# A three-layer transformer block whose instruction order is sorted with another machine model

## The chip, the cores and the metric

The kernel runs on one core of a Trainium2 chip. The metric is the time of one execution on the device, in microseconds (us). A core has five engines that work side by side, each with a queue of its own that it serves in order: PE (matrix products, fed by the weight loads PEld), DVE (elementwise work and reductions), ACT (functions of one operand, copies), POOL (here a few powers and fills) and SP, which issues almost all transfers from the main memory. The engines wait for each other by semaphores.

## The reference

The input is 256 tokens of width 1024. Three layers follow one another, each a mixer and a feed-forward network, all in fp32.

```python
def reference(x, c, ...):
    x = first_block(x, c, w_ada, ...)   # 1 layer
    return second_block(x, p_2, ...)    # 2 layers

# first_block
mod = silu(c) @ w_ada + b_ada                    # 6 x 1024 modulation values
mix = token_mixer(x * (1 + sc1) + sh1)           # top-64 indexer attention (8 heads) + gated convolution
x = layer_norm(ALPHA * x + g1 * mix)
ff = (silu(h @ w_gate) * (h @ w_up)) @ w_down    # h = x * (1 + sc2) + sh2, hidden width 2816
x = layer_norm(ALPHA * x + g2 * ff)

# second_block, layers i = 0 (gla_mixer) and i = 1 (diff_attn_mixer)
h = h + mixer_i(rms_norm(h))
h = h + swiglu_2(rms_norm(h))
h = h + sigmoid(rms_norm(h) @ ple_w_gate[i]) * (p[i] @ ple_w_proj[i])
```

The first mixer scores all keys for each query, keeps 64 of them and attends to these. The second is a gated linear attention in four heads with a forward and a backward direction. The third is an attention whose heads are differences of two softmaxes.

## The kernel before

The tokens stand in two tiles of 128 rows. Every large product streams its weight matrix once from the main memory in pieces of 256 to 512 KB. `stage` (L127 to L131) transfers a piece into one of 11 buffers `st` through SP's queue (L130). `gran` (L141 to L154) splits it into a high part `wh` (rounded copy on ACT, L150) and a low part `wl` (difference on DVE, L151); the pool `wp` has five buffers of each. The activations are split and transposed in the same way (class `XT`, `xh` and `xl`). `mm3` (L157 to L162) then makes three products for each pair of blocks: high by high (L159), high by low (L160), low by high (L162), accumulated in a bank of the result memory, of which the pool `psp` has four with the tag mm and four with the tag acc. Small transposes go through PE as well (L124).

The program runs through these stages: the modulation and the first projections (`block1`, `piece`, `both_cols`), the top-k selection in eight rounds of maxima on DVE with convolution products set between the rounds, the first attention (`attn_p`, `attn_t`, `attn_o`), the output product and the layer norm, then `ffn` (gate and up, then down, in 11 chunks of 256 columns), `gla`, `tail_layer` with a second `ffn`, `diff`, and `tail_layer` with a third `ffn`. In `diff`, `heads` (L1202 and following) makes for each pair of heads the scores (L1208), their row maximum (L1211), the scaled negative of it (L1214), the exponentials (L1217) and the difference of the two softmaxes (L1224); the source sets these calls by hand between the parts of the projections. `diff_consts` (L1075 and following), called in the second `ffn`, loads the four vectors `lv` and makes the factor `nlam` of them (L1082 to L1088).

The order of the instructions is not the order of the source. `tile.TileContext` records the instructions and sorts them when it is left: it plays the program through on a model of the machine, and whenever the model can take an instruction for an engine, it gets, of those whose inputs are done and for whose output a buffer is free, the one that stands first in the source (one block of `block1` has a higher priority). So the model decides which instruction passes which, and which buffer a tile gets. On the chip each engine then serves its queue in the order that came out, and waits where an input is not there yet. The default model is the one of the library's functional simulator.

## Time and profile before

| | us |
|---|---|
| median of 3 runs | 1054.07 (1052.72 to 1056.53) |
| profiled execution | 1055.7 |
| its span, from the first instruction to the last | 1053.9 |
| PE busy | 1015.8 (96%) |
| PEld busy | 811.2 (77%) |
| DVE busy | 636.7 (60%) |
| ACT busy | 554.8 (53%) |
| POOL busy | 49.5 (5%) |

Matmuls overlap in the records: in the third feed-forward network 840 of them, most recorded with some 390 ns each, fill 184 us. A busy PE is therefore not PE at its fastest, and a PE that is idle in the records has lost time in any case. The granted clock tells at which of its two levels PE ran. DMA share is the mean busy share of the 16 transfer engines.

### The profile page before, as it was taken

The page shows a single profiled execution, that of the slowest core. Times are in us where ns is not written, and L with a number is a line of the kernel's source. Part 1 is how long each engine was busy: PE and PEld are TensorE (multiplying, and loading weights), DVE is VectorE, ACT ScalarE, POOL GpSimd, SP SyncE. Part 2 cuts the span into 40 slices and gives each one's busy share as a digit, 9 for nine tenths or more (in the row PEclk, how much of TensorE's full clock was granted, in tenths as well). Part 3 has the DMA queues.
Part 4 walks back from the last instruction along what each step waited for, and adds up shares of the span by engine and source line. Part 5 has one row for each costly group of instructions (what it writes and reads, how often), then busy time and mean ns, then how long its engine had stood idle before and what let it go on. Part 6 is the DMA issues. An engine that isn't in the chain of part 4 may idle for free.

```text
span 1053.9 us, 13554 instructions
## 1 busy us (share of the span) xinstructions
PE 1015.8 (96%) x4883; PEld 811.2 (77%) x4883; DVE 636.7 (60%) x1043; ACT 554.8 (53%) x895; POOL 49.5 (5%) x43
## 2 busy tenths in 40 slices
PE   6889999999999999998999999999998999999998
PEld 3666675888888778886888888888676788888886
DVE  2378468654556476556555556578786665555654
ACT  2355446544445477464544446566857554444643
POOL 0000100000000000000000000004040100000000
PEclk9999999999999999999999999999999999999999
DMA  9957587966657255254665667445443466666601
GB/s 292 395 202 264 219 306 226 293 195 183 195 182 225 60 183 180 80 166 144 205 190 184 186 195 262 143 134 169 129 126 104 127 204 192 183 191 186 240 0 40
DMA packets 131783, 194.48 MB, mean 185 GB/s; under 512 B 10578, under 2 KB 93662, under 8 KB 131716
## 3 DMA queue, kind: packets, MB, share of 16 engines
q1 hardware_dynamic: 130936, 193.21, 57.4%
q10 hardware_dynamic: 780, 0.40, 0.2%
q8 instruction: 38, 0.62, 0.2%
q14 instruction: 29, 0.24, 0.1%
HBM read 192.53 MB, written 1.05 MB: 184 GB/s over the span
## 4 chain that ended last, share of the span: by engine, by line
PE 82%; DVE 7%; ACT 4%; DMA 3%; issue 2%; POOL 1%; SPq 0%; ACTq 0%; DVEq 0%; POOLq 0%
PE mmb L162 17%; PE mmb L159 17%; PE mmb L160 17%; PE acb L162 7%; PE acb L159 7%; PE acb L160 7%; DVE wl L151 2%; PE mmb L124 2%; PE acb L124 1%; POOL rs L276 1%; PE acb L337 1%; ACT wh L150 1%; DMA st<-in_w_ada_dram 1%; ACT e L1217 1%; PE mmb L337 1%
## 5 line engine op out<-in xcount | busy, mean ns | idle before, releaser
L151 DVE TENSOR_TENSOR wl<-st,wh 128x1024 fp32r<-128x1024 f32 (+4 forms) x292 | 350.9, 1206 | 233.2 <-ACT wh L150 232.4
L150 ACT CAST wh<-st 128x1024 fp32r<-128x1024 f32 (+4 forms) x292 | 300.7, 1037 | 281.9 <-PE mmb L162 141.8
L159 PE MATMUL mmb<-wh,xh 128*128 128x512 f32 (+4 forms) x888 | 352.7, 399 | 6.8 <-ACT xh L390 4.5
L160 PE MATMUL mmb<-wl,xh 128*128 128x512 f32 (+4 forms) x888 | 347.1, 392 | 2.8 <-DVE wl L151 2.8
L162 PE MATMUL mmb<-wh,xl 128*128 128x512 f32 (+4 forms) x888 | 342.3, 391 | 1.5 <-DVE xl L184 0.6
L159 PEld LDWEIGHTS mmb<-wh,xh 128*128 128x128 f32 x888 | 169.2, 191 | 44.4 <-ACT xh L390 6.3
L162 PEld LDWEIGHTS mmb<-wh,xl 128*128 128x128 f32 x888 | 169.4, 191 | 39.5 <-DVE xl L191 3.1
L160 PEld LDWEIGHTS mmb<-wl,xh 128*128 128x128 f32 x888 | 169.5, 191 | 34.6 <-DVE wl L151 3.3
L159 PE MATMUL acb<-wh,hh 128*128 128x512 f32 x216 | 84.0, 389 | 0.0
L160 PE MATMUL acb<-wl,hh 128*128 128x512 f32 x216 | 84.0, 389 | 0.0
L162 PE MATMUL acb<-wh,hl 128*128 128x512 f32 x216 | 66.6, 389 | 0.0
L159 PEld LDWEIGHTS acb<-wh,hh 128*128 128x128 f32 x216 | 40.6, 188 | 8.4
L162 PEld LDWEIGHTS acb<-wh,hl 128*128 128x128 f32 x216 | 40.5, 188 | 8.4
L160 PEld LDWEIGHTS acb<-wl,hh 128*128 128x128 f32 x216 | 40.5, 188 | 8.4
L878 POOL TENSOR_TENSOR rsx<-rsx,mhalf 128x1 f32<-128x1 f32 x12 | 10.8, 899 | 467.2 <-DVE rsx L877 467.2
L824 ACT ACTIVATE sg<-mmb,rsx 128x256 f32<-128x256 f32 x44 | 20.7, 474 | 22.2 <-PE mmb L162 20.4
L276 POOL TENSOR_TENSOR rs<-rs,mhalf 128x8 f32<-128x8 f32 (+1 forms) x14 | 20.0, 1434 | 240.7 <-DVE rs L275 240.7
L151 DVE TENSOR_TENSOR wxl<-st,wxh 128x1024 fp32r<-128x1024 f32 x22 | 26.7, 1219 | 3.0 <-ACT wxh L150 3.0
L825 DVE SCALAR_TENSOR_TENSOR sg<-mmb,rsx,sg 128x256 f32<-128x256 f32 x44 | 20.8, 480 | 11.1 <-ACT sg L824 11.1
L150 ACT CAST wxh<-st 128x1024 fp32r<-128x1024 f32 x22 | 22.7, 1051 | 5.0 <-PE acb L162 3.0
L874 ACT ACTIVATE junk<-x 128x1024 f32<-128x1024 f32 x10 | 10.6, 1059 | 25.3 <-DVE x L867 23.8
L831 DVE TENSOR_TENSOR hl<-mmb,hh 128x512 fp32r<-128x512 f32 x33 | 22.6, 684 | 1.8 <-ACT hh L830 1.8
(311 smaller groups left out, 1065.7 us busy)
## 6 DMA issues: line engine op xcount, KB each, us to landing
st<-in_ffn_w_in_dram SPq DMA_DIRECT2D x176, 256.0 KB, 3.4
st<-in_ffn_w_out_dram SPq DMA_DIRECT2D x44, 512.0 KB, 4.0
st<-in_w_ada_dram SPq DMA_DIRECT2D x32, 512.0 KB, 5.2
st<-in_diff_w_in_dram SPq DMA_DIRECT2D x24, 512.0 KB, 4.0
st<-in_w_gate_dram SPq DMA_DIRECT2D x44, 256.0 KB, 4.6
st<-in_w_up_dram SPq DMA_DIRECT2D x44, 256.0 KB, 3.1
st<-in_w_down_dram SPq DMA_DIRECT2D x22, 512.0 KB, 3.8
st<-in_w_ada_dram SPq DMA_DIRECT2D x32, 256.0 KB, 5.3
```

Of the source, the lines that this page charges most:

```text
L124: T.transpose(o, i, ident)
L150: A.copy(h[:, :n], src)
L151: V.tensor_sub(l[:, :n], src, h[:, :n].bitcast(F32))
L159: T.matmul(p_, xh, wh, start=start, stop=False)
L160: T.matmul(p_, xh, wl, start=False, stop=False)
L162: T.matmul(p_, xl, wh, start=False, stop=stop)
L276: G.tensor_tensor(r[:, :n], r[:, :n], mhalf[:, :n], op=OP.pow)
L337: T.matmul(bk[32 * j:32 * j + 32, :n], cB[:, kb, :], sts[kb // k][:, kb % k * n:kb % k * n + n], start=kb < 4, stop=kb >= 4)
L824: A.activation(sg, ps[t][:, 0:256], AF.Silu, scale=rs[t])
L825: V.scalar_tensor_tensor(sg, ps[t][:, 256:512], rs[t], sg, op0=OP.mult, op1=OP.mult)
L831: V.tensor_sub(hl, tv, hh.bitcast(F32))
L878: G.tensor_tensor(r, r, mhalf[:, 0:1], op=OP.pow)
```

## The change

The context is opened with a switch that sets the model on which the scheduler plays the program: the library's simulation in time (TimelineSim), which prices instructions, queues and transfers with another set of laws than the default. Nothing else differs: the same instructions, the same transfers, the same pools and priorities.

```diff
@@ -1344,7 +1344,7 @@
         aps[n] = nc.dram_tensor(f"in_{n}_dram", a.shape, mybir.dt.from_np(a.dtype), kind="ExternalInput").ap()
     o = nc.dram_tensor("out_0_dram", (1, S, D), F32, kind="ExternalOutput").ap()
-    with tile.TileContext(nc) as tc:
+    with tile.TileContext(nc, schedule_with_timeline_sim=True) as tc:
         body(tc, aps, o)
     r = _run(nc, [arrays], core_ids=[0])
```

## Rows read from the trace of the kernel before

**Rows 1.** The page: span, and each engine's busy us, share and instructions.
```profile
span 1053.9 us, 13554 instructions
PE 1015.8 (96%) x4883; PEld 811.2 (77%) x4883; DVE 636.7 (60%) x1043; ACT 554.8 (53%) x895; POOL 49.5 (5%) x43
```

**Rows 2.** Busy us (and instructions) by stage: start:end, length, engines, clock, DMA.
```profile
0.00:26.00 26.00, 16.91 (x94) 9.64 (x94) 5.86 (x17) 6.67 (x11) 1.68 (x7) 1.00 0.92 291
26.00:184.00 158.00, 145.97 (x799) 103.09 (x799) 104.05 (x254) 79.09 (x156) 9.02 (x6) 0.97 0.77 269
184.00:342.00 158.00, 158.00 (x716) 130.51 (x715) 89.11 (x94) 77.01 (x94) 0.00 (x0) 1.00 0.68 213
342.00:500.00 158.00, 152.90 (x755) 125.70 (x754) 99.90 (x193) 93.68 (x156) 7.45 (x10) 0.98 0.44 137
500.00:685.00 185.00, 185.00 (x843) 152.45 (x843) 105.47 (x117) 92.46 (x118) 1.93 (x2) 1.00 0.63 194
685.00:843.00 158.00, 150.98 (x751) 120.50 (x751) 116.37 (x229) 106.17 (x231) 27.43 (x16) 0.99 0.43 132
843.00:1027.00 184.00, 184.00 (x840) 151.74 (x839) 103.24 (x113) 89.88 (x111) 0.54 (x1) 1.00 0.55 171
1027.00:1054.00 27.00, 22.04 (x97) 17.58 (x95) 12.72 (x30) 9.85 (x23) 1.46 (x1) 0.98 0.11 39
```

**Rows 3.** The same view of three stretches with the lower granted clock.
```profile
46.00:49.40 3.40, 3.40 (x11) 2.82 (x10) 2.02 (x4) 2.35 (x3) 0.00 (x0) 0.50 1.06 409
...
482.90:486.30 3.40, 3.40 (x10) 2.64 (x9) 0.34 (x1) 0.00 (x0) 0.00 (x0) 0.50 0.85 280
797.00:800.30 3.30, 3.30 (x9) 2.52 (x8) 1.93 (x8) 2.82 (x11) 0.00 (x0) 0.50 0.26 92
```

**Rows 4.** Waits of PE: who waited for whom, us in total, times, longest.
```profile
PE mmb L159 <- ACT xh L390: 4.5, 2, 2.6
PE mmb L160 <- DVE wl L151: 2.8, 2, 2.5
...
PE acb L124 <- DVE r L1188: 1.6, 2, 1.3
PE acb L124 <- ACT e L1217: 1.5, 1, 1.5
```

**Rows 5.** Instructions in order of time, 470 to 482 us: start, length, [idle before].
```profile
475.56 0.29 DVE L1082 TENSOR_TENSOR lp<-lv 128x128 f32<-128x128 f32 x1 [4.88 <-DMA lv<-in_diff_lam_k_dram]
475.77 1.22 DVE L151 TENSOR_TENSOR wl<-st,wh 128x1024 fp32r<-128x1024 f32 x1
...
477.21 0.20 ACT L1085 ACTIVATE l<-l 128x2 f32<-128x2 f32 x1 [3.76 <-DVE l L1084]
477.32 1.98 ACT L150 CAST wh<-st 128x1024 fp32r<-128x1024 f32 x2
...
481.36 0.50 PE L160 MATMUL mmb<-wl,xh 128*128 128x512 f32 x1 [2.45 <-DVE wl L151]
```

**Rows 6.** Chain of waits of 737 to 843 us, share of that stretch by line.
```profile
by line: DVE wl L151 15.9%; issue 9.4%; PE mmb L159 8.4%; ACT e L1217 8.4%; PE mmb L162 7.6%; PE mmb L160 7.0%; POOL rs L276 5.0%; ACT wh L150 4.8%; PE acb L1208 4.1%; DMA st<-in_ffn_w_out_dram 3.3%; DVE mx L1211 2.9%; PE acb L124 2.8%; DVE
```

**Rows 7.** Groups by line, 737 to 843 us: xcount | busy us, mean ns | idle before.
```profile
L151 DVE TENSOR_TENSOR wl<-st,wh 128x1024 fp32r<-128x1024 f32 x24 | 29.1, 1218 | 1.5 <-ACT wh L150 1.3
L150 ACT CAST wh<-st 128x1024 fp32r<-128x1024 f32 x24 | 24.9, 1049 | 7.7 <-PE mmb L162 7.2 <-ACT xh L183 0.5
...
L1211 DVE TENSOR_REDUCE mx<-acb 128x2 f32<-128x512 f32 x16 | 10.6, 684 | 5.0 <-PE acb L1208 4.9
```

**Rows 8.** Busy us of each engine, 737 to 843 us, columns as in rows 2.
```profile
737.00:843.00 106.00, 98.98 (x511) 78.01 (x510) 75.89 (x153) 72.38 (x172) 15.71 (x10) 0.98 0.41 123
```

**Rows 9.** DVE and ACT in order of time, 742 to 746 us.
```profile
742.56 0.69 DVE L1211 TENSOR_REDUCE mx<-acb 128x2 f32<-128x512 f32 x1 [2.45 <-PE acb L1208]
743.17 1.22 DVE L151 TENSOR_TENSOR wl<-st,wh 128x1024 fp32r<-128x1024 f32 x1
744.30 0.15 DVE L1214 SCALAR_TENSOR_TENSOR mx<-mx,rq 128x2 f32<-128x2 f32 x1
...
744.55 1.28 ACT L1217 ACT_TABLE_LOAD   x1 [1.43 <-DVE mx L1214]
```

**Rows 10.** Waits of the transfer queue (SPq): us in total, times, longest.
```profile
SPq L130 <- DVE wl L151: 497.9, 221, 24.5
```

## The prediction

> **What bounds the kernel now.** I read the page first: TensorE (PE) is busy 1015.8 of 1053.9 us, DVE 60% and ACT 53% [rows 1]. That names the engine, not the places, so the second view was the table by stage. It splits the span in two halves of almost the same length. In three stages (184 to 342, 500 to 685 and 843 to 1027 us, the three feed-forward networks, 527 us together) PE is busy for every microsecond [rows 2]. In the other five PE is idle for 9.1, 12.0, 5.1, 7.0 and 5.0 us, 38.2 in all [rows 2]. The first is the wait for the first data and the last the final normalisation; no order of the queues removes much of them. The three in the middle, 24.1 us, hold the top-k attention, the gated linear attention and the differential attention. There the work goes round from PE to DVE, ACT and Pool and back.
>
> A second cost sits in the same stages. Behind the start, PE runs six times at the lower of its two clock levels (1.2 GHz, granted clock 0.50) for about 3.4 us; the first, the fifth and the last of the six stand in [rows 3]. The stage table shows 1.00 in all three full stages [rows 2]. The fifth, at 482.9, begins 1.5 us after a wait of PE of 2.45 us has ended [rows 3, 5]. A full stage runs 843 matmuls in 185 us, 15.5 in 3.4 us; the fifth stretch ran 10 [rows 2, 3]. At 4.56 matmuls per us one such stretch costs (15.5 - 10) / 4.56 = 1.2 us, and 1.7 if all of its 3.4 us are halved. I take 1.5, six of them 9 us.
>
> Third I asked what makes PE late. The list of its waits is short: single pauses of 1 to 3 us behind ACT and DVE [rows 4]. Fourth, the order of time shows how one comes about [rows 5]: DVE stands 4.88 us at the first use of lv, whose transfer is late, and ACT 3.76 us for the result. The weight splits L150 and L151 queue behind both, and PE waits 2.45 us for a wl. A queue is served in the order in which the scheduler wrote it. Fifth, the chain of waits of 737 to 843 us: DVE's L151 has 15.9% of it and ACT's L150 4.8%, so 16.9 + 5.1 = 22.0 of its 106 us are weight splits [rows 6].
>
> **The change part by part.** It removes and adds no instruction and no transfer. It makes the scheduler's clock another one, so what moves is the order in each engine's queue, and which buffer a tile gets, hence which release it waits for. All engines' queues, SP's with the weight transfers included, are dealt anew.
>
> *Full stages.* PE has no pause in 527 us, DVE is at 56 to 57% and ACT at 49 to 50% [rows 2]. The order may change here and should cost 0: PE's own sum stays. The cover is the supply of split weights; it would be gone only if DVE or ACT ran full.
>
> *SP's queue.* The weight transfers wait above all for buffers: 497.9 us in 221 waits for a DVE split to release one [rows 10]. A transfer issued in another place would mostly have stood there anyway, so 0. At the start, where the DMA share is 0.92 [rows 2], the same bytes come through the same engines; I put 0 here too, with 2 us to either side.
>
> *The dependent stages, loss.* A split is ready as soon as its weights have landed; a step of a chain is ready only when the step before is done. A scheduler that hands out what is ready gives splits the free moments between two steps. The trace has the pattern: between the row maximum L1211 and its 0.15 us continuation L1214 DVE runs a 1.22 us split, and ACT, which needs the L1214, waits 1.43 us [rows 9]. A simulation of the whole program may offer more such moments, wherever it tells the end of an engine's work from the arrival of its result. No row shows what it will do, so I bound it. Upwards: all splits of 737 to 843 us, 29.1 + 24.9 = 54.0 us [rows 7], come to lie on the chain instead of 22.0. PE's pauses there are 7.0 us (106 - 98.98) [rows 8], 0.32 us for each us of split on the chain. So 32.0 more make 10.2 us in this stage, and by the ratio of the pauses (24.1 / 7.0 = 3.4) 35 us in all three; with three more slow-clock stretches, 40 us. Downwards: none more, 0. The value: one split more ahead of each of the 8 blocks of scores (16 maxima, two a block) [rows 7], 8 x 1.22 = 9.8 us on the chain, 3.1 us of pauses, x 3.4 = 10.5 us, and two more slow-clock stretches, 3.0. Sum 13.5 us. It is nearer to the lower end because only the maxima stand as a proven place.
>
> *The dependent stages, gain.* A machine that tells late transfers and slow steps better puts the splits ahead of the blocked instruction. What that can give back: the pause at 481 and its slow clock, 2.45 + 1.5 = 4.0 us [rows 3, 5], and at most the 7.0 us of pauses of 685 to 843 us with one slow stretch, 8.5 [rows 2, 3]. Together 12.5; the outer bound is all 24.1 us with all six stretches, 33. Against the full 12.5 speaks that much of it is true dependence: PE waits for an exponential or a normalised row that has just been made [rows 4]. I take half, 6.3 us.
>
> *Sum.* 13.5 - 6.3 = 7.2 us. The profiled execution took 1055.7 us, of which 1053.9 are its span and 1.8 lie around it; it becomes 1062.9. It stands 1.6 above the median of the three runs, 1054.07, to which the same 7.2 us are added: 1061.
>
> On headroom the Trainium skill says something else than the page's first line (Perfetto Trace Analysis, Identifying the Most-Contended Engine): matmul busy time misjudges how near PE is to its limit because matmuls are pipelined, and the share of weight loads is the better measure. This trace bears it out in part: weight loads fill 0.825 of the full stages and 0.714 of the other five (376.5 of 527 us) [rows 2]. By PE's busy time the room is 38.2 us; by that measure it is 527 - 376.5 / 0.825 = 71 us. The third rival is built on it.
>
> **The rivals.** *Better order* (faster). The new clock is nearer to the chip, queue heads block less, and the 12.5 us come back with no new splits on the chain: 1041.6. For it: the block at 472 to 481 us is a plain error of forecast, and DVE and ACT have idle time enough to do everything sooner. Against: the source interleaves its stages by hand, and the order of the queues is this fine; the few pauses left are mostly single microseconds. It decides if fewer than 22 us of splits lie on the chain of 737 to 843 us.
>
> *No change that shows.* The queues of DVE and ACT are redealt, but PE's order and its pauses stay, or gains and losses cancel; or the switch does not reach the order at all. 1054. For it: half of the span is full, and 0.3%, about what a measurement of this kernel can tell from no change, is 3.2 us. Against: the middle stages turn on steps of 0.2 to 1.2 us, and a redeal that leaves all pauses equal would be chance.
>
> *Large room* (faster). Pauses are not all: matmuls within the thin stages also run thinner than in the full ones, by the weight loads 71 us against 38. If a better order packs a third of it, 23.5 us, the time is 1030.5. For it: 26 to 184 us alone has 158 - 103.09 / 0.825 = 33 us of this room [rows 2]. Against: that stage is full of the short products of the modulation, the top-k rounds and the attention, whose loads and products don't pace as the large ones do.
>
> **How the numbers follow.** Forecast (more splits ahead of the chains, slower) 0.47; better order 0.28; no change 0.19; large room 0.06. The predicted time is the forecast's, 1061. Faster by over 0.3% is 0.28 + 0.06 = 0.34, within 0.19, slower 0.47. The forecast's own range goes from 1057, where slower begins to show, to 1088, the upper bound of 40 us less the 6.3 of gain. As cases of both signs hold most of the chance, the whole range reaches down to 1037, half of the outer gain of 33 us below the median; beyond lie most of the large room below and a rest of the loss above.
>
> **What would show it.** Right: after the change the three full stages are still without a pause and take 527 us; PE's busy time stays near 1016; in the differential attention the chain of waits has more than 20.7% of L150 and L151 together, PE's pauses in the three middle stages add up to some 30 us or more, and there are more than six slow-clock stretches. Wrong: pauses of PE in a full stage (then a buffer, not an order, went wrong, and the loss has no bound from here); a wait of PE at its first weights longer than now; or DVE's 4.88 us at lv gone with the split share of the chain no larger, which is the better order. The weakest step is the count of eight more splits: nothing in the trace fixes it.

## The result and the profile after

The kernel became slower: 1083.56 us (1081.16 to 1085.41) against 1054.18 of the kernel before beside it, a ratio of 1.0271 with an interval of 1.0245 to 1.0296. That is 29 us more; the forecast was 7 more. The time lies inside the range given and the direction was the likeliest case; the size is four times the forecast's.

The page comes first: the span, the busy time of each engine (share, instructions) and one group of PE's products by the low part `wl`, with its idle time at the end.

```profile
span 1079.4 us, 13556 instructions
...
PE 1030.4 (95%) x4883; PEld 821.3 (76%) x4883; DVE 637.8 (59%) x1043; ACT 555.8 (51%) x895; POOL 43.4 (4%) x43
...
L160 PE MATMUL mmb<-wl,xh 128*128 128x512 f32 (+4 forms) x888 | 347.5, 392 | 0.0
```

Against [rows 1] PE is busy for 14.6 us more with the same 4883 matmuls, and idle for 49.0 us (1079.4 - 1030.4) where it was 38.1. The two add up to 25.5 us, the whole difference of the two spans. DVE, ACT and the weight loads did not become a bound. The last line shows that no pause is left behind a split of DVE; before, there was the one of 2.45 us [rows 4, 5].

The stage table (start:end, length, busy us and count of PE, PEld, DVE, ACT, POOL, granted clock, DMA share, GB/s), with the borders of [rows 2]:

```profile
0.00:26.00 26.00, 16.82 (x89) 9.84 (x90) 6.23 (x18) 6.70 (x11) 1.68 (x7) 1.00 0.90 289
26.00:184.00 158.00, 147.48 (x761) 99.79 (x760) 99.28 (x244) 73.72 (x147) 8.33 (x6) 0.92 0.76 267
...
342.00:500.00 158.00, 152.96 (x755) 127.88 (x754) 94.11 (x171) 89.69 (x140) 4.68 (x8) 0.97 0.42 130
...
685.00:843.00 158.00, 146.79 (x712) 117.15 (x711) 112.11 (x218) 101.63 (x208) 23.43 (x14) 0.96 0.43 132
```

The start has not changed (16.82 against 16.91 us busy). The work of the later stages has slid behind these borders, so it is the clock column that is to be read: 0.92, 0.97 and 0.96 in the stages with attention where it was 0.97, 0.98 and 0.99 [rows 2]. The same view of three stretches of the old length inside the feed-forward networks:

```profile
200.00:358.00 158.00, 158.00 (x716) 130.53 (x715) 88.35 (x92) 74.71 (x91) 0.00 (x0) 1.00 0.64 199
510.00:695.00 185.00, 184.30 (x836) 152.00 (x835) 104.16 (x117) 90.30 (x115) 0.00 (x0) 1.00 0.63 198
860.00:1044.00 184.00, 183.30 (x833) 151.13 (x832) 104.19 (x117) 92.83 (x118) 0.55 (x1) 1.00 0.55 177
```

Here nothing happened: 525.6 us busy of 527.

So the loss is in the stages that depend on a chain, in two forms. The waits of PE (who for whom, total, times, longest) show the first, pauses:

```profile
PE acb L124 <- ACT x L794: 6.1, 3, 2.6
PE acb L124 <- DVE e L1224: 5.7, 3, 2.8
...
PE acb L124 <- DVE ao L354: 3.0, 1, 3.0
```

All that are shown are transposes (L124) of something that an attention or a norm has just finished, where [rows 4] has single waits of 1 to 3 us. The second form is the clock. The same table for all stretches behind the start in which PE ran at the lower of the two levels (1.2 GHz):

```profile
59.60:63.00 3.40, 3.04 (x8) 2.58 (x9) 3.03 (x4) 1.56 (x4) 0.00 (x0) 0.50 1.05 407
121.00:127.80 6.80, 6.80 (x30) 5.93 (x30) 4.72 (x6) 2.89 (x7) 0.00 (x0) 0.50 0.50 156
131.30:141.50 10.20, 8.01 (x38) 6.55 (x42) 5.42 (x10) 3.28 (x8) 4.36 (x3) 0.50 0.36 103
179.00:182.40 3.40, 3.40 (x18) 0.86 (x10) 2.80 (x7) 2.55 (x7) 0.56 (x1) 0.51 0.40 112
192.70:196.10 3.40, 3.40 (x9) 2.65 (x8) 3.40 (x5) 2.12 (x3) 0.00 (x0) 0.50 0.42 131
383.90:394.10 10.20, 8.56 (x26) 7.35 (x27) 8.93 (x13) 6.01 (x14) 0.18 (x2) 0.50 0.24 74
827.60:834.40 6.80, 5.71 (x23) 3.37 (x22) 3.97 (x10) 5.04 (x15) 0.00 (x0) 0.50 0.25 77
837.80:844.60 6.80, 4.80 (x23) 4.83 (x24) 1.96 (x5) 0.88 (x4) 0.00 (x0) 0.50 0.00 0
```

They last 51.2 us together (51.0 by these rounded rows), as much as fifteen of the stretches of 3.4 us of which there were six before, 20.5 us [rows 3]. Before 200 us they take 27 us where it was 10, in the gated linear attention 10 where it was 7, and in the differential attention 14 where it was 3.

How the two come about is seen in PE's own order. These are PE's instructions in the last 30 us of the differential attention (start, length, count, idle before):

```profile
820.95 2.10 PE L1208 MATMUL acb<-kT,qT 64*128 64x256 f32 x16
822.98 0.73 PE L162 MATMUL mmb<-wh,xl 128*128 128x512 f32 x2
827.26 0.41 PE L124 MATMUL acb<-ident,e 128*128 128x128 f32 x2 [3.54 <-ACT e L1217]
827.60 2.09 PE L1208 MATMUL acb<-kT,qT 64*128 64x256 f32 x8
...
831.39 1.09 PE L124 MATMUL acb<-ident,e 128*128 128x128 f32 x4 [1.09 <-DVE e L1224]
...
836.21 0.74 PE L124 MATMUL acb<-ident,e 128*128 128x128 f32 x4 [1.71 <-DVE e L1224]
839.80 0.66 PE L124 MATMUL acb<-ident,e 128*128 128x128 f32 x2 [2.85 <-DVE e L1224]
...
848.52 0.66 PE L124 MATMUL acb<-ident,od 128*128 128x128 f32 x4 [1.81 <-DVE od L1257]
```

And the corresponding stretch of the kernel before:

```profile
801.55 1.14 PE L1208 MATMUL acb<-kT,qT 64*128 64x256 f32 x8
802.62 0.50 PE L159 MATMUL mmb<-wh,ph 128*128 128x512 f32 x1
...
805.52 0.60 PE L124 MATMUL acb<-ident,e 128*128 128x128 f32 x4
806.05 1.14 PE L1208 MATMUL acb<-kT,qT 64*128 64x256 f32 x8
807.58 0.74 PE L124 MATMUL acb<-ident,e 128*128 128x128 f32 x4 [0.40 <-DVE e L1224]
808.08 0.48 PE L159 MATMUL mmb<-wh,xh 128*128 128x512 f32 x1
```

Before, each eight scores (L1208) of this stretch are followed, at most with a transpose between, by three or four us of large products (L159 to L162) that need nothing from the attention; while PE works on them, DVE and ACT make the exponentials and differences that the next transposes want. After, sixteen scores run together in 2.10 us, and from 824 to 848 us PE's queue holds nothing but steps of the chain. Each waits for the one before: 3.54, 1.09, 1.71, 2.85, 1.81 us. The clock falls 0.3 us after the first of these pauses has ended, and 8 score products then take 2.09 us, where 16 had taken 2.10. The large products that should stand between had been served earlier: up to the first score of the stage (766.0 us, 741.4 before) PE had run 303 of them since the last hidden tile of the second feed-forward network, where it had been 277, and from there to the last product with v only 174, where it had been 193.

The first attention has the same form:

```profile
119.86 0.70 PE L649 MATMUL acb<-kT,qT 64*128 64x256 f32 x2
...
120.80 1.05 PE L649 MATMUL acb<-kT,qT 64*128 64x256 f32 x2
...
129.55 0.89 PE L124 MATMUL acb<-ident,e 128*128 128x128 f32 x4 [1.41 <-ACT e L660]
133.49 1.09 PE L124 MATMUL acb<-ident,ao 128*128 128x128 f32 x4 [3.04 <-DVE ao L354]
```

Here the clock falls at 121.0 us with no pause in the records ahead of it: since 113 us PE had served little else than scores of 64 x 256 (L649), masks and transposes. Two of these scores then take 1.05 us in place of 0.70. The waits of 1.41 and 3.04 us, at 128 and 130 us, follow, and the second slow stretch begins within the longer one.

### The profile page after: what moved, and what is told of

Its sections match the earlier page's. It is cut to its first block, busy times and chain, and to the rows that moved or that the text cites. A ratio compares the mean times of both kernels' runs of the same rounds, so it can differ in the third digit from the quotient of the medians.

```text
span 1079.4 us, 13556 instructions
## 1 busy us (share of the span) xinstructions
PE 1030.4 (95%) x4883; PEld 821.3 (76%) x4883; DVE 637.8 (59%) x1043; ACT 555.8 (51%) x895; POOL 43.4 (4%) x43
## 3 DMA queue, kind: packets, MB, share of 16 engines
HBM read 192.53 MB, written 1.05 MB: 179 GB/s over the span
## 4 chain that ended last, share of the span: by engine, by line
PE 90%; ACT 4%; DMA 3%; DVE 2%; issue 1%; SPq 0%; POOL 0%; DVEq 0%; ACTq 0%; POOLq 0%
PE mmb L159 19%; PE mmb L160 18%; PE mmb L162 18%; PE acb L159 7%; PE acb L162 7%; PE acb L160 7%; PE acb L124 2%; PE mmb L124 2%; PE mmb L337 1%; DMA st<-in_w_ada_dram 1%; PE acb L337 1%; PE acb L1208 1%; PE acb L680 1%; ACT wh L150 1%; PE acb L649 1%
## 5 line engine op out<-in xcount | busy, mean ns | idle before, releaser
L151 DVE TENSOR_TENSOR wl<-st,wh 128x1024 fp32r<-128x1024 f32 (+4 forms) x292 | 351.1, 1208 | 261.1 <-ACT wh L150 259.1
L150 ACT CAST wh<-st 128x1024 fp32r<-128x1024 f32 (+4 forms) x292 | 301.3, 1039 | 298.7 <-PE mmb L162 171.2
L159 PE MATMUL mmb<-wh,xh 128*128 128x512 f32 (+4 forms) x888 | 351.1, 398 | 8.7 <-ACT xh L390 2.8
L162 PE MATMUL mmb<-wh,xl 128*128 128x512 f32 (+4 forms) x888 | 338.7, 390 | 0.8 <-DVE xl L178 0.8
L159 PEld LDWEIGHTS mmb<-wh,xh 128*128 128x128 f32 x888 | 169.0, 191 | 49.3 <-ACT xh L390 5.0
L162 PEld LDWEIGHTS mmb<-wh,xl 128*128 128x128 f32 x888 | 167.7, 189 | 35.0 <-DVE xl L178 1.6
L159 PE MATMUL acb<-wh,hh 128*128 128x512 f32 x216 | 84.0, 389 | 0.0
L162 PE MATMUL acb<-wh,hl 128*128 128x512 f32 x216 | 66.1, 389 | 0.0
L162 PEld LDWEIGHTS acb<-wh,hl 128*128 128x128 f32 x216 | 40.6, 188 | 8.4
L159 PEld LDWEIGHTS acb<-wh,hh 128*128 128x128 f32 x216 | 40.5, 188 | 8.4
L151 DVE TENSOR_TENSOR wxl<-st,wxh 128x1024 fp32r<-128x1024 f32 x22 | 26.7, 1224 | 16.8 <-ACT wxh L150 16.5
L276 POOL TENSOR_TENSOR rs<-rs,mhalf 128x8 f32<-128x8 f32 (+1 forms) x14 | 22.7, 1622 | 281.3 <-DVE rs L275 268.7
L150 ACT CAST wxh<-st 128x1024 fp32r<-128x1024 f32 x22 | 22.8, 1048 | 19.9 <-PE acb L162 8.1
L825 DVE SCALAR_TENSOR_TENSOR sg<-mmb,rsx,sg 128x256 f32<-128x256 f32 x44 | 21.1, 481 | 12.4 <-ACT sg L824 12.4
L831 DVE TENSOR_TENSOR hl<-mmb,hh 128x512 fp32r<-128x512 f32 x33 | 22.6, 685 | 4.6 <-ACT hh L830 4.6
L878 POOL TENSOR_TENSOR rsx<-rsx,mhalf 128x1 f32<-128x1 f32 x12 | 6.5, 544 | 456.0 <-DVE rsx L877 456.0
L337 PE MATMUL acb<-st,cB 128*32 128x512 f32 (+1 forms) x112 | 19.9, 659 | 2.8 <-DMA st<-in_w_ada_dram 1.9
```

Source lines behind the costliest of these rows:

```text
L150: A.copy(h[:, :n], src)
L151: V.tensor_sub(l[:, :n], src, h[:, :n].bitcast(F32))
L159: T.matmul(p_, xh, wh, start=start, stop=False)
L162: T.matmul(p_, xl, wh, start=False, stop=stop)
L276: G.tensor_tensor(r[:, :n], r[:, :n], mhalf[:, :n], op=OP.pow)
L337: T.matmul(bk[32 * j:32 * j + 32, :n], cB[:, kb, :], sts[kb // k][:, kb % k * n:kb % k * n + n], start=kb < 4, stop=kb >= 4)
```

## The experiments

The diff changes one argument, so what can be varied is the order that comes out. Two edits do that. The first limits how far the simulation in time lets one engine's queue run ahead: how many instructions the scheduler may hand to that engine before the simulated engine has done the earlier ones. It is 35 for PE and 12 for the others. The second pins an engine's queue to the order of another kernel: an edge without a semaphore between each instruction and its successor in a list of places.

```diff
+    from concourse.hw_specs import TRN2Spec as spec
+    spec.ENG_ISSUE_QUEUE_DEPTH = {**spec.ENG_ISSUE_QUEUE_DEPTH, mybir.EngineType.PE: N}
     with tile.TileContext(nc, schedule_with_timeline_sim=True) as tc:
         body(tc, aps, o)
```

```diff
+def _pin(tc, engine, ranks):
+    mine = [i for i in tc.nc.cur_bb.bb.instructions if i.engine == engine and type(i).__name__ != "BassTilePoolBoundary"]
+    info = mybir.DependencyInfo(mybir.DependencyClass.NoSync, mybir.DependencyReason.DATA)
+    for a, b in zip(ranks, ranks[1:]):
+        tc.add_manual_dep(mine[b], mine[a].name, info, reason="pinned order")
...
         body(tc, aps, o)
+        for e, ranks in _ORDER.items():
+            _pin(tc, getattr(mybir.EngineType, e), ranks)
```

The theories: the loss is made by the order in PE's queue, because a deep simulated queue hands the independent products out too early; or by the orders of DVE, ACT and SP; or by the buffers that the simulation chose. All kernels compute the whole reference.

| kernel | what differs | us | ratio to before, 95% |
|---|---|---|---|
| e6_window4 | changed kernel, PE 4 ahead | 1058.46 | 1.0030 [1.0008, 1.0051] |
| e10_window8 | PE 8 ahead | 1055.77 | 0.9994 [0.9970, 1.0019] |
| e4_window12 | PE 12 ahead | 1064.39 | 1.0079 [1.0054, 1.0103] |
| e9_window20 | PE 20 ahead | 1065.94 | 1.0094 [1.0065, 1.0123] |
| the changed kernel | PE 35 ahead | 1083.56 | 1.0271 [1.0245, 1.0296] |
| e12_others1 | PE 35, the others 1 | 1080.69 | 1.0229 [1.0187, 1.0271] |
| e1_window1 | PE 1 ahead | 1168.41 | 1.1068 [1.1041, 1.1096] |
| e5_tl_all_before | simulation in time, all five orders of before | 1057.52 | 1.0023 [0.9996, 1.0049] |
| e11_def_all_after | default model, all five orders of after | 1085.59 | 1.0275 [1.0224, 1.0325] |
| e2_def_pe_after | default model, PE's order of after | 1104.24 | 1.0452 [1.0436, 1.0468] |
| e3_tl_pe_before | simulation in time, PE's order of before | 1088.22 | 1.0296 [1.0270, 1.0323] |
| e7_pe_diff | after, PE's order of before in `diff` alone | 1076.49 | 1.0199 [1.0160, 1.0239] |
| e8_pe_block1 | after, PE's order of before in `block1` alone | 1083.30 | 1.0279 [1.0233, 1.0324] |

**The order is all of it, in both directions.** With the switch set but all queues in the order of before:

```diff
+_ORDER = {
...
+}
...
     with tile.TileContext(nc, schedule_with_timeline_sim=True) as tc:
         body(tc, aps, o)
+        for e, ranks in _ORDER.items():
+            _pin(tc, getattr(mybir.EngineType, e), ranks)
```

> The simulation in time as the scheduler's model, but all five queues (PE, DVE, ACT, Pool, SP) pinned to the order of the kernel before. What the simulation still decides is which buffer a tile gets. Theory O (the order in the queues is all that the change moves in time): 1052 to 1060 us. Theory C (buffers chosen by the other model's times make the waits): over 1065 us, up to the changed kernel's 1084.

Measured 1.0023, theory O: no loss that can be told from none; the interval leaves room for half a percent. The converse, the default model with all queues in the order of after:

```diff
+_ORDER = {
...
+}
...
-    with tile.TileContext(nc, schedule_with_timeline_sim=True) as tc:
+    with tile.TileContext(nc) as tc:
```

> The scheduler's default model chooses nothing of the order here: all five queues are pinned to the changed kernel's order; only the choice of buffers is left to it. If the order in the queues is the whole of the change, the loss comes back whole: about 1083 us, ratio 1.027. If the buffers that the simulation in time chooses carry a part of the loss, it stays below 1078 us.

Measured 1.0275: the whole loss. Span and busy time of that kernel, from its page:

```profile
span 1083.5 us, 13557 instructions
...
PE 1032.2 (95%) x4883; PEld 822.4 (76%) x4883; DVE 637.8 (59%) x1043; ACT 556.3 (51%) x895; POOL 43.5 (4%) x43
```

PE's busy time and idle time (51.3 us) are those of the changed kernel within 2.3 us. The choice of buffers carries nothing that shows.

**One queue alone.** The default model with PE's order of after, and the simulation in time with PE's order of before, the other queues dealt anew in both:

```diff
+_ORDER = {
+    "PE": [
...
-    with tile.TileContext(nc, schedule_with_timeline_sim=True) as tc:
+    with tile.TileContext(nc) as tc:
```

> The kernel before with its own scheduler model, but PE's instructions pinned to the order that they have in the changed kernel; DVE, ACT, Pool and SP are sorted by the default model. Theory A: 1073 to 1090 us, the whole slowdown with nothing but PE's order. Theory B: 1050 to 1062 us.

```diff
+_ORDER = {
+    "PE": [
...
     with tile.TileContext(nc, schedule_with_timeline_sim=True) as tc:
```

> The changed kernel with PE's instructions pinned to the order of the kernel before; all other queues are sorted by the simulation in time. Theory A: 1048 to 1060 us. Theory B: 1073 to 1088 us.

Measured 1.0452 and 1.0296 (1104.24 and 1088.22 us): each mixture is at least as slow as the pure kernels. The first lies above both theories' ranges; the second misses theory A and stands just at the upper end of theory B's (A: PE's order makes the loss; B: the other engines' orders and the buffers do). PE's order of after comes with a loss here too, but PE's order of before takes none away. One of PE's waits in the second kernel, 1.5 us in the kernel before and 3.0 in the changed one:

```profile
PE acb L124 <- DVE ao L354: 4.4, 1, 4.4
```

Their reading is that an order of PE is good only with the queues that feed it. These two runs therefore don't say which queue carries the loss. The sharper mixture, PE's order of one kernel with all other queues of the other, was not run.

**How far PE's queue runs ahead.** With N = 1:

> The changed kernel, with one number of the scheduler's simulation set back: how many instructions it lets PE's queue take ahead of the one that runs, 1 instead of 35. The program that comes out lets 148 of 4563 PE instructions pass an older one; the changed kernel 1383, the kernel before 322. Theory A (the slowdown comes from PE's order: ready matmuls are handed out far ahead, and a step of the attention that becomes ready stands behind them): 1046 to 1060 us, slow-clock stretches back to about six. Theory B (it comes from the other engines' order and from buffers chosen by other times): 1073 to 1085 us, since the simulation and its times stay.

This missed altogether: 1168.41 us. A simulated PE that takes one instruction at a time hardly lets anything pass. Counted in PE's instruction lists, 148 instructions stand ahead of an older one of the source, against 322 in the kernel before and 1383 after. The waits are long, even in the feed-forward networks (sg):

```profile
PE acb L124 <- DVE e L1224: 17.9, 5, 5.1
PE mmb L124 <- DVE sg L825: 16.0, 2, 8.1
```

So 1 is not less of the same cause; PE is idle there for 112.7 us (1165.5 - 1052.8), and little passes anything. The doses between stand for the question:

> The changed kernel with 4 in place of 35 for the number of instructions that the simulation lets PE's queue take ahead; 543 PE instructions pass an older one (148 at 1, 829 at 12, 1383 at 35). Theory A (a longer look ahead is worse, and the run at 1 is bad only because the simulated PE then can't overlap its instructions): 1050 to 1066 us, as good as 12 or better. Theory F (PE needs to be filled by passing instructions, and fewer passes are worse): between the runs at 1 and at 12, 1075 to 1150 us.

> TensorE's modelled queue takes at most 8 instructions ahead, all else is the changed kernel. If the depth sets the loss: between the 1058.5 us of depth 4 and the 1064.4 us of depth 12, about 1061 us. If single orders scatter by several microseconds whatever the depth, it can fall below 1055 us, the time of the kernel before, or above 1066.

> As the run with the window of 1, with 12 in its place: 829 PE instructions pass an older one. Theory A: between the two, 1058 to 1075 us. Theory B: 1073 to 1085 us, as with any window.

> TensorE's modelled queue takes at most 20 instructions ahead (35 in the changed kernel), all else is the changed kernel. If the depth sets the loss (4: 1058.5 us, 12: 1064.4, 35: 1083.6), this lies between the last two: by a straight line between them 1064.4 + 8/23 x 19.2 = 1071 us, with a slow-clock time behind the start between 20 and 51 us. If the 1083.6 us is an accident of one order and the depth doesn't order the times, it can fall anywhere from 1055 to 1085; a time outside 1064 to 1084 speaks for that.

From 4 to 35 the count of passing instructions is 543, about 790, 829, about 990 and 1383 (for 8 and 20 an estimate from the order of PE's records in their traces, which comes out within 50 of the other three), and the ratio 1.0030, 0.9994, 1.0079, 1.0094, 1.0271. Between the steps 8, 12 and 35 the intervals don't touch; 4 and 8 lie within half a percent in the wrong order, 4 and 12 came out in theory A's ranges, and 8 and 20 both some 5 us below the straight line that was expected. So the depth sets the size of the loss, with a scatter of a few us by the single order. In each of these kernels the other queues are dealt anew as well, so the runs show PE's depth in the simulation as the cause, and not the order of PE's queue by itself. With 4 ahead the page reads like that of before:

```profile
span 1053.1 us, 13584 instructions
...
PE 1015.5 (96%) x4883; PEld 813.5 (77%) x4883; DVE 635.8 (60%) x1043; ACT 555.7 (53%) x895; POOL 48.7 (5%) x43
```

PE's busy time is 1015.5 and its idle time 37.6 us, and its slow-clock time behind the start 20.5 us as before. From 20 to 35 the slow-clock time goes from 20.5 to 51.2 us and PE's busy time from 1019.6 to 1030.4; this last step is most of the loss (18 of 29 us). At 12 and 20 PE is busy for 5.3 and 3.8 us more than before without more slow clock. Two groups of short products take longer there, with the same count: the modulation's (L337, 28.5 us before, 37.2 and 32.8 in these two) and the first attention's scores (L649, 4.8 us before, 7.1 and 6.8). They take longer where the order breaks them up. At 12 ahead two products of L337 alone fill 1.04 us, and twelve together 1.91:

```profile
116.44 1.04 PE L337 MATMUL mmb<-st,cB 128*32 128x512 f32 x2
...
122.20 1.91 PE L337 MATMUL mmb<-st,cB 128*32 128x512 f32 x12
```

In the same way two scores (L649) fill 0.70 us in the changed kernel, as shown above, where the kernel before runs four in 0.70 us at 112.4 us. No run varied this alone.

The other engines' depth, with PE left at 35:

```diff
+    spec.ENG_ISSUE_QUEUE_DEPTH = {e: (n if e == mybir.EngineType.PE else 1) for e, n in spec.ENG_ISSUE_QUEUE_DEPTH.items()}
```

> The other engines' modelled queues (12 deep in the changed kernel) take 1 instruction ahead, TensorE's stays at 35. If TensorE's depth alone carries the loss: about 1084 us, at least 1075. If the depth of the vector and scalar engines' queues carries a part of it, the time comes down towards 1065 us or less. If the loss comes from the order in which ready steps are handed out to whichever engine, it may also rise, as it did with depth 1 on TensorE (1168 us): above 1100 us.

Measured 1.0229 (1080.69 us). Most of the loss stays: the run-ahead of DVE, ACT and SP carries at most a small part, and the two intervals overlap.

**Where in the program.** The changed kernel with the 556 instructions of PE in `diff`, or the 655 in `block1`, pinned to the order of before:

```diff
+_ORDER = {
+    "PE": [
...
     with tile.TileContext(nc, schedule_with_timeline_sim=True) as tc:
```

> The changed kernel with only the 556 PE instructions of the differential attention pinned to their order in the kernel before; everything else is sorted by the simulation. Theory A (steps of the attention stand too late on PE): the stage gives back its 10 us, 1069 to 1077 us, and the six pauses at its end, 11.8 us together, shrink to under 6. Theory M (orders of the engines belong together, and a pinned PE meets queues that are not made for it): 1078 to 1090 us.

> The changed kernel with only the 655 PE instructions of the first block up to its layer norm pinned to their order in the kernel before. Theory A: the block gives back its part of the loss, 1066 to 1076 us. Theory M: 1080 to 1092 us, as in the run with all of PE pinned, where this block was 18 us longer than before.

The first gave back 7 us (1076.49, theory A, near the upper end of its range). The end of the attention, in the columns of the stage table, in the changed kernel and then in this one:

```profile
817.00:851.00 34.00, 22.07 (x109) 16.59 (x108) 19.18 (x45) 18.57 (x57) 2.01 (x2) 0.80 0.20 63
```

```profile
790.00:850.00 60.00, 54.91 (x293) 44.05 (x293) 41.67 (x79) 39.47 (x101) 11.08 (x7) 1.00 0.39 116
```

Idle time of PE fell from 11.9 in 34 us to 5.1 in 60, and the 13.7 us of slow clock there are gone. So in this stage it is shown that PE's order, the pauses and the slow clock go together. Other small pauses came elsewhere: over the whole execution PE's idle time is 48.5 us against 49.0, and what came back is slow clock (34.1 us behind the start against 51.2).

The second gave nothing in time (1083.30, theory M). PE's old order there met queues of DVE and ACT that were not made for it; its longest such wait is longer than the 3.0 us that it was to remove:

```profile
PE acb L124 <- DVE ao L354: 4.5, 1, 4.5
```

But the clock followed PE's order here too. The first attention in the changed kernel and then in this one:

```profile
113.00:150.00 37.00, 32.53 (x166) 23.37 (x166) 23.09 (x51) 19.59 (x47) 6.27 (x4) 0.77 0.57 194
```

```profile
113.00:150.00 37.00, 31.57 (x226) 21.16 (x224) 25.04 (x56) 20.32 (x45) 6.59 (x4) 0.99 0.65 234
```

The 17 us of slow clock are down to one stretch of 6.8 us, which begins at 149.4 us within that wait of 4.5 us, and PE runs 226 products in the time in which it had run 166. Over the whole execution PE is busy for 5.4 us less than in the changed kernel and idle for 6.7 us more, and the slow clock comes to the same 51.2 us, as the differential attention has 20.5 of it here and had 13.7: pauses and a longer slow stretch elsewhere took what the first attention gave.

## Why the prediction had the sign right, and the mechanism and the size wrong

*Full stages at 0 and SP's queue at 0* held. The feed-forward networks have no pause worth naming; the start is equal to 0.1 us; SP still waits above all for DVE's splits (475.5 us in 221 waits, 497.9 before [rows 10]).

*The loss: more splits ahead of the chain's steps.* This step failed. The sign came out, but by another mechanism, so as a forecast of the splits it was luck. The forecast said that with the loss the splits L150 and L151 would take more than 20.7% of the chain of waits in the differential attention [rows 6]. The same chain of the changed kernel, over 106 us again:

```profile
by line: PE mmb L159 18.0%; PE mmb L160 17.4%; PE mmb L162 17.1%; PE acb L124 9.4%; PE acb L1208 8.7%; PE acb L1245 6.6%; ACT e L1217 3.9%; DVE mx L1211 2.4%; ACT sq L1255 2.3%; issue 2.0%; DVE e L1224 1.4%; ACT xh L183 1.2%; DVE wl L151 1.
```

L151 has under 2%, and L150, not among the lines shown, has no more than that: the splits left the chain. What stands on it is PE: the large products with 52.5% (23.0 before), and the transposes, scores and products with v with 24.7%. The prediction's reason was that a scheduler which hands out what is ready gives the free moments to what never waits. The runs on the depth bear that out, but the thing that never waits was looked for in DVE's queue only. On PE it is the large products. Served early, they stand ahead of the chain: from the last hidden tile of the second feed-forward network (L831, done at 671.9 us before and 690.2 after) to the first score (L1208, 741.4 and 766.0 us) it now takes 75.8 us in place of 69.5, with 26 large products more. And then they are used up, so that at the stage's end nothing is left to cover the chain.

*The size.* The loss had 10.5 us of pauses and 3.0 of slow clock (two stretches). Of the gain of 6.3, which is half of 12.5, 4.8 are pauses and 1.5 slow clock, as the 12.5 hold two stretches. So PE's idle time was to rise by 10.5 - 4.8 = 5.7 us and rose by 10.9, and the slow clock was to add 3.0 - 1.5 = 1.5 to PE's busy time, which rose by 14.6. The 18.3 us that were missing (25.5 - 7.2) are 5.2 of the first and 13.1 of the second. The term that was most mis-sized is the count of slow-clock stretches: nine more, where two came in with the loss and one went out with the gain. At the 1.5 us each of the prediction nine make 13.5 us, near the 14.6. The price was about right and the count was not, because the stretches were thought of as single ones behind single pauses, where a run of chain steps with nothing between them goes with a lower clock for 7 to 10 us at a time. Not all of the 14.6 need be clock: e8_pe_block1 has the same 51.2 us of it and is busy for 5.4 us less. The price has a check in e5_tl_all_before, which has the order of before in every queue. Its page:

```profile
span 1059.9 us, 13554 instructions
...
PE 1021.7 (96%) x4883; PEld 814.1 (77%) x4883; DVE 636.6 (60%) x1043; ACT 555.0 (52%) x895; POOL 47.3 (4%) x43
```

This execution was longer than that of before by 6.0 us with the same idle time (38.2 us), and had 34.1 us of slow clock behind the start, as much as ten such stretches in place of six: 5.9 us of busy time for four, 1.48 us each. The runs that were not profiled agree: each has its mean granted clock on record, and the four of the changed kernel have 0.970 to 0.975, where 42 of the kernel before have 0.984 to 0.997, 0.989 in the mean. At some 0.9 us for each 0.001, as the last section has it, the difference of 0.016 is 14 us of the 29, an estimate.

*The gain of 6.3.* PE's pause behind lv, with its stretch, is gone, worth 4.0 us by the prediction's own rows, but DVE stands there as before:

```profile
492.60 0.29 DVE L1082 TENSOR_TENSOR lp<-lv 128x128 f32<-128x128 f32 x1 [4.19 <-DMA lv<-in_diff_lam_k_dram]
```

So the block did not go as the prediction had it; PE only no longer waits behind it. None of the rest came: the pauses of the differential attention grew instead.

*The rivals.* No kernel with another order was faster than before by more than its interval, so the better order and the large room found nothing to bear them out. The test that was to tell the better order, under 22 us of splits on the chain, was met by a kernel that is slower: it asked about DVE's queue, and the loss lay in PE's. The Trainium skill's measure by the share of weight loads (Perfetto Trace Analysis, Identifying the Most-Contended Engine) puts the room at 71 us by the prediction's estimate; the share fell here from 0.770 to 0.761 of the span, 811.2 of 1053.9 and 821.3 of 1079.4, which goes with the slower time, but no run recovered any of that room.

*Of the signs of being right*, three came: the full stages at 525.6 us busy of 527, pauses of 32.7 us in the three stages between (12.4, 7.1 and 13.2, from 26 us on and outside the three stretches above), and more slow clock than six stretches. Two failed: PE's busy time near 1016, and the share of the splits on the chain. Of the signs of being wrong none came beyond 1.4 us of pauses in the full stages, so they could not have told that the mechanism was another one.

## What to carry to other kernels

On an engine that is nearly full, work that needs nothing is the cover of the work that waits: look in its own queue for stretches in which only steps of one chain follow each other, because that is where pauses and the lower clock come together. When the order of a scheduler changes, count how far instructions pass each other and on which engine, then vary that one depth, rather than judge the model as a whole. Look also at short products that ran in groups: broken up, they take PE longer with the same count. The orders of the queues belong together: to test an order, pin all of them, since a queue of one order among queues of another can be slower than both.

## What the runs showed of the hardware

The same order of all queues had 20.5 us of slow clock in one profiled execution and 34.1 in another, whose spans lie 6 us apart. The 16 runs of the kernel before beside the last experiments spread from 1050.2 to 1061.2 us, and the clock goes with that scatter: the mean granted clock was 0.995 in the fastest and 0.984 in the slowest, and over the 16 the time rises by about 0.9 us for each 0.001 that the clock falls (correlation -0.96). A stretch of 3.4 us at half the clock is 0.0016 of the span, so 1.4 us by this. Why one order gets more such stretches in one execution than in another stays open.

The clock also fell without any recorded pause of PE, at 121.0 us of the changed kernel, after eight us of short attention products and transposes. PE counts as busy there, but it ran few products; the same eight us in the changed kernel and in the kernel before, where the clock stayed up:

```profile
113.00:121.00 8.00, 8.00 (x35) 4.90 (x35) 3.58 (x14) 5.14 (x15) 0.00 (x0) 1.00 0.66 248
```

```profile
113.00:121.00 8.00, 8.00 (x68) 5.64 (x66) 5.02 (x13) 4.25 (x13) 0.13 (x1) 1.00 0.23 66
```
